# Weight-row requests placed one product later, from the input products to the first projection

## The chip, the cores and the metric

The kernel runs on one core of a Trainium2 chip. The metric is device time of one execution, in microseconds (us), as the median of several runs. A profile is one execution recorded by the hardware's profiler: when every instruction of every engine began, how long it took and which semaphore released it. Engines are named as in the profile: PE is TensorE (matmul), DVE is VectorE, ACT is ScalarE, POOL is GpSimd, SP is SyncE, which here issues nearly all DMAs from one queue.

## The reference

One layer of a hybrid decoder block on x of 1024 tokens by 1024 channels, in float32:

```
xn = rmsnorm(x)
qa, ka, va, qr, kr, vr, gr, gate_a, gate_b = xn @ w_in      (split by columns)
o_a = dilated windowed attention of 12 heads, mixed in 4 slots by their softmax denominators
o_r = groupnorm(retention(qr, kr, vr)) * silu(gr)
y   = sigmoid(gate_a) * (o_a @ w_proj_a) + sigmoid(gate_b) * (o_r @ w_proj_b)
x   = x + y @ w_out
x   = x + square(relu(rmsnorm(x) @ w_up)) @ w_down
```

Everything is to float32 accuracy, so each matmul of two float32 operands is made as three: each operand is split into a high part (a rounded copy) and a low part (the rest), and high x high, high x low and low x high are summed in PSUM.

## The kernel before

The stages follow one another in time: the values (`w_av`), the input products (36 units of `w_in`: 12 of query/key columns, 8 of the retention's gate, 8 of the mixers' gates, 8 of the retention's query/key columns), with the attention of the 12 heads woven into the second half of them; retention, 4 heads of 8 chunks each, with `w_rv`; the first projection (`w_pa`), 16 items, two for each of 8 weight units; the second (`w_pb`), 8 units; `w_out`; the MLP up and down.

**Products.** A unit of the input weight is a matrix of 1024 by 256, multiplied by a form of Strassen's algorithm: seven products N1 to N7, each 12 matmuls of 128x128 by 128x512 (four row blocks times three). They need four pieces of the unit: A (for N1 and N2), B (N6, N3), C (N5, N7) and D (N4). `strassen_order` (L364) lists the products; in the steady part unit j has N6(j), N1(j+2), N5(j), N7(j), N2(j+2), N4(j), N3(j).

**Weights.** Class `Weights` (L68) carries all weights from memory to split pieces. A *row* is one request of 512 KB (256 KB for `w_pa`) into a raw place of SBUF; there are three or four places, taken in turn (`place`). A *step* is one split of a raw row, or a part of it, into high and low part: a copy on ACT (L431) and a subtraction on DVE (L434). A unit has two rows. Its steps are A from the first row, D from the second, four sums of quarters within the raw rows (L159), then B from the first row and C from the second; B and C are the last users of their rows, and mark them in `used`. Over the units the order of steps is A(j+1), D(j), B(j), C(j) (L164 to L174).

**When a step is traced.** `Pipe.step` traces a product's matmuls and then calls `tick` (L304), which counts the clock up and, with `pace` 1, takes one step through `pump` (L270). A step is taken only if the pieces that were in its buffer before are done (`free` marks them after their last product), if its row was requested, and if the clock stands at least `lag` ticks after that row's request (`born`, L278). After each step `pump` calls `load` (L251) until it says no. `load` requests the next row in order if the row that had its place before is in `used`. The product's evacuations from PSUM, and the stores they lead to, are traced after the tick.

In retention, `pace` is None: steps are taken when a weight is freed, in the last chunk of each head, whose product is longer (24 matmuls). From the end of the last chunk on, `lag` is 2 and `pace` 1 again (L1392). In the first projection a tick comes after each of the 16 items: 12 matmuls, then a pinned sigmoid of the next item's gate (L1412), the multiplication of the gate with the sum in PSUM (L1413) and a store (L1414). The item's sum takes one of three banks (`ms`). `split_halves` and `load_half` bring in the operands of the second projection meanwhile.

**What sets the order on the engines.** The PE's order is the program's. For the others a planner of the compiler places the instructions in a simulated time: it takes what it holds to be ready, the earlier traced first. An instruction passed to `keep_in_program_order` is pinned: it is issued behind the instruction that was traced just before it on its engine. Pinned are, among others, the attention's fetches on SP (`late`, L1015: L1023, L1030, L1032, L1046, and L552) and the sigmoids of the gates on ACT (L1215). Requests of rows (L265) are not pinned. A queue is in order: an instruction of SP that waits for a semaphore holds what is behind it.

Of the kernel before, what the change touches and what calls it, by code (L numbers as in the profile page):

```python
# [67 lines left out]
class Weights:  # L68
# [12 lines left out]

    def __init__(self, nc, rawp, wp, split):
        self.nc, self.rawp, self.wp, self.split = nc, rawp, wp, split
        self.raw, self.used, self.next = [], set(), 0
        self.src, self.steps = [], []
        self.place, self.more = [], None
        self.last = {}
        self.units, self.done = {}, set()
        self.plain = self.taken = 0
        self.cycle, self.turn = tuple(range(self.WB)), 0  # L90

        self.places = {}
        self.limit, self.keep, self.first = None, None, {}
        self.clock, self.lag, self.pace, self.every, self.born = 0, 0, None, 1, []

    def claim(self, buf, key):

# [10 lines left out]
    def add(self, src, buf=None, pin=False):  # L108

        n = self.plain  # L110
        if buf is None:
            buf = self.cycle[self.turn % self.WB]
            self.turn += 1
        r = len(self.src)
        self.src.append(src)
        self.place.append(n % 6 if n < 8 else (n - 4) % self.RAW)
        w = src.shape[1]
        cuts = [slice(0, w // 2), slice(w // 2, w)] if n < 3 else [slice(0, w)]

        def step():  # L120
            h, l = self.buffer(buf)
            for c in cuts:
                self.split(h[:, c], l[:, c], self.raw[r][:, c], pin)
            self.units[n] = h, l
            self.used.add(r)

        self.steps.append((self.claim(buf, n), r, step))
        self.plain += 1

    def add_units(self, tag, srcs, flip=0):  # L130

        base = len(self.src)
        self.first[tag] = len(self.steps)
        kept = {}
        for s in srcs:
            self.place += [(len(self.src) + i - base) % (self.RAW + 1) for i in range(2)]
            self.src += [s[1], s[0]]

        def piece(key, buf, r, cols, then=None):
            def step():  # L140
                if isinstance(buf, tuple):
                    if not kept:
                        kept["D"] = self.buffer(buf[0])
                    h, l = (x[:, 512 * buf[1]:512 * buf[1] + 512] for x in kept["D"])
                else:
                    h, l = self.buffer(buf)
                late = key[0] == "pb" and key[1] > 1
                self.split(h, l, self.raw[r][:, cols], late or key[0] == "up" and key[1] < 2 and key[2] != "A")
                self.units[key] = h, l
                if then:  # L150
                    then()

            self.steps.append((self.claim(buf, key), r, step))

        def sums(r, which=(0, 1, 2, 3)):
            (x22, x21), (x11, x12) = ((self.raw[i][:, 0:512], self.raw[i][:, 512:1024]) for i in (r, r - 1))
            for k in which:
                x, y = ((x22, x21), (x21, x11), (x11, x22), (x12, x11))[k]
                ins = self.nc.vector.tensor_tensor(x, x, y, op=OP.add)  # L159
                if tag == "up" and r <= base + 3:  # L160
                    self.keep(ins)

        both = slice(0, 1024)
        for j in range(-1, len(srcs)):  # L164
            if j + 1 < len(srcs):
                piece((tag, j + 1, "A"), self.A[(j + 1) % 2], base + 2 * (j + 1), both)
            if j >= 0:
                r = base + 2 * j + 1
                fine = tag == "pb" and j > 1
                piece((tag, j, "D"), (self.D, j % 2), r, slice(0, 512), None if fine else lambda r=r: sums(r))  # L170
                if fine:
                    self.steps += [(set(), r, lambda r=r, k=k: sums(r, k)) for k in ((0, 1), (2, 3))]
                piece((tag, j, "B"), self.B[(j + flip) % 2], r - 1, both, lambda r=r: self.used.add(r - 1))
                piece((tag, j, "C"), self.C, r, both, lambda r=r: self.used.add(r))  # L174
        m = len(srcs) + flip
        self.cycle = (0, 1, self.B[m % 2], self.C, self.D, self.B[(m - 1) % 2])
        self.turn = 0

    def add_values(self, tag, quarters):

        base = len(self.src)
        w11, w12, w21, w22 = quarters
        self.src += [w[h] for h in range(2) for w in (w22, w21, w11)] + [*w12, *w22]
        self.place += [0, 1, 2, 3, 4, 5, 0, 3, 1, 4]

        def add(x, y):
            self.nc.vector.tensor_tensor(self.raw[x], self.raw[x], self.raw[y], op=OP.add)

        def piece(name, h, buf, r, ends=(), plus=None):
            key = (tag, name, h)  # L190

            def step():
                if plus is not None:
                    add(r, plus)
                hl = self.buffer(buf)
                self.split(*hl, self.raw[r])
                self.units[key] = hl
                self.used.update(ends)

            self.steps.append((self.claim(buf, key), r, step))  # L200

        rows = [range(base + 3 * h, base + 3 * h + 3) for h in range(2)]
        for r22, r21, r11 in rows:
            for x, y in ((r22, r21), (r21, r11), (r11, r22)):
                self.steps.append((set(), r11, lambda x=x, y=y: add(x, y)))
        for h, (r22, r21, r11) in enumerate(rows):
            piece("N6", h, 2 + h, r11)
        for h, (r22, r21, r11) in enumerate(rows):
            piece("N5", h, 4 + h, r22, (r22,))
        for h, (r22, r21, r11) in enumerate(rows):  # L210
            piece("N7", h, h, r21, (r21,))
        for h, (r22, r21, r11) in enumerate(rows):
            piece("N3", h, 2 + h, base + 6 + h, (base + 6 + h, r11), r11)
        for h in range(2):
            piece("N4", h, 4 + h, base + 8 + h, (base + 8 + h,))

    def add_chunks(self, tag, srcs, buffers):


        for c, quarters in enumerate(srcs):  # L220
            base = len(self.src)
            self.place += [(base + i) % (self.RAW + 1) for i in range(4)]
            self.src += quarters
            x00, x10, x11, x01 = range(base, base + 4)
            for name, r, other, op, ends in (
                    ("N1", x00, None, None, ()), ("N2", x10, None, None, ()), ("N3", x11, None, None, ()),
                    ("N5", x00, x01, OP.subtract, ()), ("N7", x01, x11, OP.subtract, (x01,)),
                    ("N6", x11, x00, OP.add, (x00,)), ("N4", x10, x11, OP.subtract, (x10, x11))):
                buf, key = buffers[c % 2][name], (tag, c, name)

                def combine(r=r, other=other, op=op, pin=c > 0):
                    ins = self.nc.vector.tensor_tensor(self.raw[r], self.raw[r], self.raw[other], op=op)
                    if pin:
                        self.keep(ins)

                def step(r=r, ends=ends, buf=buf, key=key, pin=c > 0):
                    h, l = self.buffer(buf)
                    self.split(h, l, self.raw[r], pin)
                    self.units[key] = h, l
                    self.used.update(ends)  # L240

                if other is not None:
                    self.steps.append((set(), x01, combine))
                self.steps.append((self.claim(buf, key), x01, step))
# [6 lines left out]
    def load(self, queues=None):  # L251
# [1 line left out]
        if n >= min(len(self.src), self.hold):  # L253
            return False
        b = self.place[n]
        if any(self.place[m] == b and m not in self.used for m in range(max(0, n - 12), n)):
            return False
        if b >= self.RAW and self.more is None:
            return False
# [30 lines left out]

    def __getitem__(self, i):
        while i not in self.units:
            lag, self.lag, at = self.lag, 0, self.next
            self.pump(1)
            self.lag = lag
            assert self.next > at
        return self.units[i]

# [5 lines left out]
    def tick(self):  # L304
        self.clock += 1
        if self.pace is not None and self.clock % self.every == 0:
            self.pump(self.pace)


class Pipe:  # L310
# [67 lines left out]
def hybrid_block(ctx: ExitStack, tc: tile.TileContext, a: dict, out: bass.AP):  # L378
# [727 lines left out]
    with ExitStack() as ph:  # L1106
# [77 lines left out]

        unit = {}
        NIN = NA + NG + NQ + 8
        W.lag, W.pace = 2, 1
        first = W.take(4)
        for p, (j, name) in enumerate(strassen_order(NIN, True)):
            if p == FIRST - 4:  # L1190
# [204 lines left out]
    with ExitStack() as ph:  # L1395
# [108 lines left out]
        fetched = {order[order.index(at) - 3]: u for at, u in free.items()}  # L1504
        todo, unit, base = [(0, "N3", h) for h in range(2)], {}, len(work)

        W.lag = 3
        fetch(0)
        fetch(1)
        sigmoid(ahead[0][0])  # L1510
# [440 lines left out]
```

## Time and profile before

| | |
|---|---|
| median of 3 runs | 2157.25 us (2156.55 to 2160.52) |
| the profiled execution | 2157.57 us, its span 2155.7 us |
| PE, DVE, ACT, POOL busy | 99%, 64%, 52%, 15% of the span |
| DMA | 366.14 MB, mean 170 GB/s |
| rows requested | 202 (L265) |
| SP's time ahead of row requests, put down to the split on DVE (L434) | 473.0 us, 123 times |

The span runs from the first to the last instruction of the program; the time of the run has some 1.9 us more. A row of a timeline gives the start, the duration, the engine, the line, the operation, what it writes and reads, and in square brackets the idle time before it with what ended it. A row of the waits gives who waited for whom: total, times, longest. A row of the chain of waits gives start, duration and what held the end of the program back at that time. A row of busy time by stage gives the stage, then busy time and number of instructions of PE, PE's weight loads, DVE, ACT, POOL, then the granted clock of PE, the share of the DMA engines and GB/s. All times are in us.

### The profile page before, as it was taken

How to read it: one execution, taken by the hardware profiler on the slowest of the kernel's cores; microseconds unless marked ns; L12 is line 12 of the kernel's file. 1: busy time of each engine (PE TensorE's matmuls, PEld its weight loads, DVE VectorE, ACT ScalarE, POOL GpSimd, SP SyncE). 2: the span in 40 equal slices, each digit the busy share in tenths (PEclk: the TensorE clock that was granted, in tenths of full speed). 3: DMA queues.
4: the chain of work that ended last, by engine and by line, in shares of the span. 5: the costliest groups of instructions: out<-in, count | busy, mean ns of one | idle time of the engine just before them, and what ended most of it. 6: DMA issues, size and time to landing. Idle time of an engine off the chain costs nothing.

```text
span 2155.7 us, 28537 instructions
## 1 busy us (share of the span) xinstructions
PE 2135.5 (99%) x9840; PEld 1751.6 (81%) x9840; DVE 1381.2 (64%) x2352; ACT 1117.2 (52%) x2149; POOL 312.7 (15%) x340
## 2 busy tenths in 40 slices
PE   9999999999999999999999999999999999999999
PEld 7887777888888888888888877778788888788887
DVE  7944434655556565667867777783865556788884
ACT  8534555435555554445555655542655545755552
POOL 1000000000000000003123110000000000777773
PEclk9999999999999999999999999999999999999999
DMA  8433333333667666665354586864254556745443
GB/s 328 152 113 98 109 106 99 106 135 134 197 199 214 196 206 192 209 190 167 110 169 138 156 295 228 277 235 142 84 169 141 155 161 191 238 155 192 159 142 107
DMA packets 296336, 366.14 MB, mean 170 GB/s; under 512 B 35120, under 2 KB 202480, under 8 KB 295936
## 3 DMA queue, kind: packets, MB, share of 16 engines
q1 hardware_dynamic: 295648, 364.06, 53.7%
q8 instruction: 77, 1.26, 0.2%
q14 instruction: 67, 0.55, 0.1%
q10 hardware_dynamic: 544, 0.26, 0.0%
HBM read 247.67 MB, written 116.59 MB: 169 GB/s over the span
## 4 chain that ended last, share of the span: by engine, by line
PE 84%; DVE 5%; DMA 5%; ACT 2%; issue 2%; POOL 1%; SPq 0%; DVEq 0%; POOLq 0%; ACTq 0%
PE mm L327 44%; PE ms L327 32%; PE ms L782 2%; PE tr L997 1%; PE tr L976 1%; PE mm L782 1%; DMA xl<-on_d 1%; DMA s<-sg_d 1%; DVE wl L434 1%; PE tr L987 1%; PE tr L1344 1%; DVE xl L434 1%; PE tr L1129 1%; DVE raw L159 1%; PE ms L1284 1%
## 5 line engine op out<-in xcount | busy, mean ns | idle before, releaser
L434 DVE TENSOR_TENSOR wl<-raw,wh 128x1024 fp32r<-128x1024 f32 (+1 forms) x305 | 338.2, 1110 | 405.2 <-ACT wh L431 404.0
L431 ACT ACTIVATE wh<-raw 128x1024 fp32r<-128x1024 f32 (+1 forms) x305 | 291.6, 959 | 286.0 <-PE ms L327 93.9
L327 PE MATMUL mm<-xh,wh 128*128 128x512 f32 x960 | 388.1, 404 | 3.0 <-ACT ms L504 1.7
L327 PE MATMUL mm<-xh,wl 128*128 128x512 f32 x960 | 375.1, 391 | 0.8 <-DVE wl L434 0.7
L327 PE MATMUL mm<-xl,wh 128*128 128x512 f32 x960 | 374.1, 390 | 0.8 <-DVE xl L434 0.8
L327 PE MATMUL ms<-xh,wh 128*128 128x512 f32 x784 | 318.1, 406 | 4.0 <-ACT u L512 1.6
L327 PE MATMUL ms<-xh,wl 128*128 128x512 f32 x784 | 306.2, 391 | 0.5 <-DVE wl L434 0.5
L327 PE MATMUL ms<-xl,wh 128*128 128x512 f32 x784 | 305.6, 390 | 0.0
L327 PEld LDWEIGHTS mm<-xh,wl 128*128 128x128 f32 x960 | 180.2, 188 | 40.9 <-DVE wl L434 1.9
L327 PEld LDWEIGHTS mm<-xh,wh 128*128 128x128 f32 x960 | 180.5, 188 | 38.8 <-ACT ms L504 2.5
L327 PEld LDWEIGHTS mm<-xl,wh 128*128 128x128 f32 x960 | 180.7, 188 | 35.2 <-DVE xl L434 1.3
L327 PE MATMUL mm<-wh,xh 128*128 128x512 f32 x474 | 192.3, 406 | 0.0
L327 PE MATMUL mm<-wh,xl 128*128 128x512 f32 x474 | 185.6, 392 | 0.0
L327 PE MATMUL mm<-wl,xh 128*128 128x512 f32 x474 | 184.8, 390 | 0.0
L327 PEld LDWEIGHTS ms<-xh,wh 128*128 128x128 f32 x784 | 147.4, 188 | 44.9 <-issue 10.1
L1317 POOL TENSOR_TENSOR st<-st,half 128x1 f32<-128x1 f32 x32 | 25.3, 790 | 1038.6 <-DMA at<-acc_d 882.2
L327 PEld LDWEIGHTS ms<-xh,wl 128*128 128x128 f32 x784 | 147.1, 188 | 32.9 <-DVE wl L434 1.0
L327 PEld LDWEIGHTS ms<-xl,wh 128*128 128x128 f32 x784 | 147.6, 188 | 27.0
L327 PEld LDWEIGHTS mm<-wh,xl 128*128 128x128 f32 x474 | 89.0, 188 | 19.9
L327 PEld LDWEIGHTS mm<-wh,xh 128*128 128x128 f32 x474 | 89.2, 188 | 16.6 <-ACT ms L1761 0.6
L327 PEld LDWEIGHTS mm<-wl,xh 128*128 128x128 f32 x474 | 89.4, 189 | 16.2
L159 DVE TENSOR_TENSOR raw<-raw,raw 128x512 f32<-128x512 f32 x120 | 83.6, 697 | 3.0
(360 smaller groups left out, 3822.0 us busy)
## 6 DMA issues: line engine op xcount, KB each, us to landing
raw<-in_w_up SPq DMA_DIRECT2D x32, 512.0 KB
h_d<-s SPq DMA_DIRECT2D x64, 256.0 KB
raw<-in_w_down SPq DMA_DIRECT2D x32, 512.0 KB
xl<-on_d SPq DMA_DIRECT2D x28, 512.0 KB
raw<-in_w_aqk_q SPq DMA_DIRECT2D x24, 512.0 KB
qk_d<-sg SPq DMA_DIRECT2D x48, 256.0 KB
qk<-qk_d SPq DMA_DIRECT2D x24, 512.0 KB
rb<-rs_d SPq DMA_DIRECT2D x24, 512.0 KB
```

Of the source, the lines that this page charges most:

```text
L159: ins = self.nc.vector.tensor_tensor(x, x, y, op=OP.add)
L327: self.nc.tensor.matmul(ps, x, y, start=start, stop=stop, skip_group_check=not first)
L431: hi = nc.scalar.activation(dst_h, src, AF.Copy)
L434: lo = nc.vector.tensor_tensor(dst_l, src, dst_h.bitcast(F), op=OP.subtract)
L782: nc.tensor.matmul(pm, x, w, start=k == m == 0, stop=k == n - 1 and m == 2)
L976: nc.tensor.matmul(sp[:, to], q, qk[c][:, 1, (n0 - 4 * c) * P:(n1 - 4 * c) * P], start=True, stop=True)
L987: nc.tensor.transpose(tp[:, j], st["p"][:, j * P:(j + 1) * P], ident)
L997: nc.tensor.matmul(po, st["t"][:, j], V[k // 2][:, k % 2], start=(j == 0), stop=(j == nk - 1))
L1129: nc.tensor.matmul(to[m:m + 32], pick[:, 31 - n:63 - n], x, start=n == 0, stop=n == HEADS - 1)
L1284: nc.tensor.matmul(sp[:, :P], kT[:, f], qT[:, f], start=(f == 0), stop=(f == 1))
L1317: nc.gpsimd.tensor_tensor(st[:, 9:10], st[:, 8:9], half[:, 0:1], op=OP.pow)
L1344: nc.tensor.transpose(pt[:, f, :], it["o"][:, f * P:(f + 1) * P], ident)
```

## The change

`Weights` gets a number `rest`. `used`, which was a set of rows whose last split was traced, becomes a table of the clock at which that was (`spent`). `load` asks for the next row only when `rest` ticks have passed since the row ahead of it in its place was used up; a row still in use counts as never. `tick` requests rows after its pump as long as `rest` is not 0 and `load` grants them, since no step need follow to call it. A weight that is needed at once (`__getitem__`) sets `rest` aside, as it does `lag`. `rest` is 1 from the first input product on and 0 again from the second projection on; it is 0 before.

```
     def __init__(self, nc, rawp, wp, split):
-        self.raw, self.used, self.next = [], set(), 0
+        self.raw, self.used, self.next, self.rest = [], {}, 0, 0
...
+    def spent(self, *rs):
+        self.used.update((r, self.clock) for r in rs)
...
-            self.used.add(r)
+            self.spent(r)
...
-        if any(self.place[m] == b and m not in self.used for m in range(max(0, n - 12), n)):
+        if any(self.place[m] == b and self.used.get(m, 1 << 30) + self.rest > self.clock
+               for m in range(max(0, n - 12), n)):
             return False
...
     def __getitem__(self, i):
         while i not in self.units:
-            lag, self.lag, at = self.lag, 0, self.next
+            lag, rest, self.lag, self.rest, at = self.lag, self.rest, 0, 0, self.next
             self.pump(1)
-            self.lag = lag
+            self.lag, self.rest = lag, rest
             assert self.next > at
...
         if self.pace is not None and self.clock % self.every == 0:
             self.pump(self.pace)
+        while self.rest and self.load():
+            pass
...
         NIN = NA + NG + NQ + 8
-        W.lag, W.pace = 2, 1
+        W.lag, W.pace, W.rest = 2, 1, 1
...
-        W.lag = 3
+        W.lag, W.rest = 3, 0
         fetch(0)
```

The other four places that marked a row in `used` call `spent` in the same way.

More of the change, by code (lines that the diff above doesn't have):

```diff
@@ L172, in add_units @@
                     self.steps += [(set(), r, lambda r=r, k=k: sums(r, k)) for k in ((0, 1), (2, 3))]
-                piece((tag, j, "B"), self.B[(j + flip) % 2], r - 1, both, lambda r=r: self.used.add(r - 1))
-                piece((tag, j, "C"), self.C, r, both, lambda r=r: self.used.add(r))
+                piece((tag, j, "B"), self.B[(j + flip) % 2], r - 1, both, lambda r=r: self.spent(r - 1))
+                piece((tag, j, "C"), self.C, r, both, lambda r=r: self.spent(r))
         m = len(srcs) + flip
@@ L197, in step @@
                 self.units[key] = hl
-                self.used.update(ends)
+                self.spent(*ends)
             self.steps.append((self.claim(buf, key), r, step))
@@ L239, in step @@
                     self.units[key] = h, l
-                    self.used.update(ends)
+                    self.spent(*ends)
                 if other is not None:
```

## The prediction

> **What bounds the kernel now.** First the page's totals: TensorE is busy in 99% of the span, so time can only come from the 1% in which it waits.
>
> ```profile
> span 2155.7 us, 28537 instructions
> PE 2135.5 (99%) x9840; PEld 1751.6 (81%) x9840; DVE 1381.2 (64%) x2352; ACT 1117.2 (52%) x2149; POOL 312.7 (15%) x340
> ```
>
> Then the busy time by stage (the first pair after the span is TensorE). The change acts from the input products (about 130 us) to the start of the second projection (about 1286 us).
>
> ```profile
> 130.00:414.00 284.00, 283.95 (x1284) 223.56 (x1283) 124.63 (x157) 146.15 (x207) 0.00 (x0) 1.00 0.35 105
> 414.00:525.00 111.00, 111.00 (x493) 91.94 (x492) 68.77 (x92) 45.50 (x65) 0.00 (x0) 1.00 0.37 125
> 525.00:905.00 380.00, 378.29 (x1925) 318.68 (x1924) 226.52 (x615) 202.51 (x549) 0.00 (x0) 1.00 0.67 204
> 905.00:1225.00 320.00, 318.84 (x1548) 264.07 (x1547) 227.69 (x525) 169.15 (x356) 64.55 (x80) 1.00 0.51 149
> 1225.00:1286.00 61.00, 60.14 (x269) 48.27 (x267) 43.22 (x68) 34.96 (x57) 11.98 (x17) 1.00 0.88 290
> 1286.00:1440.00 154.00, 148.87 (x647) 120.98 (x648) 121.29 (x157) 80.43 (x112) 0.00 (x0) 1.00 0.76 253
> ```
>
> TensorE is idle 0.05 us in the products alone, 1.7 us where attention is woven in, 1.2 us in retention, and at the seam of the two projections. Third, what ended TensorE's waits: the waits of 525 to 905 us (two rows), of retention (one row), and of the seam, 1225 to 1310 us (three rows).
>
> ```profile
> PE tr L976 <- DVE acc L979: 1.4, 1, 1.4
> PE tr L976 <- DVE qk L1040: 0.3, 1, 0.3
> PE tr L1344 <- DVE on L1319: 1.1, 3, 0.6
> PE mm L327 <- ACT wh L431: 1.0, 1, 1.0
> PE mm L327 <- ACT ms L504: 0.8, 1, 0.8
> PE mm L327 <- DVE wl L434: 0.7, 1, 0.7
> ```
>
> So all that could be won in the touched stages is 1.4 + 0.3 + 1.1 + 1.0 + 0.8 + 0.7 = 5.3 us, 0.25% of the span. A loss has no such limit.
>
> **The change, part by part.** No instruction is added or removed: 94 of the 202 requests (`L265`) are traced later: 18 of the query/key rows, 16 each of `w_gr`, `w_gate`, `w_rqk` and `w_rv`, 8 of `w_pa`, 4 of `w_pb`. Each keeps its issue time on SP.
>
> *1. The products.* Counting from the code, unit j has the products N6(j), N1(j+2), N5(j), N7(j), N2(j+2), N4(j), N3(j). At the tick of N6(j) the split B(j+1) is traced and frees a place; the row for A(j+3) is requested there. At the tick of N2(j+2) the same holds for C(j+1) and the second row of unit j+3. The first request moves to the tick of N1(j+2), the second to that of N4(j). The split A(j+3) is traced at N4(j)'s tick, 5 products after its request, now 4; the lag of two ticks does not bind, so no split moves. Here is ACT (two rows), DVE and SP in one such stretch:
>
> ```profile
> 210.88 1.06 ACT L431 ACTIVATE wh<-raw 128x1024 fp32r<-128x1024 f32 x1 [1.62 <-DMA raw<-in_w_aqk_q]
> 216.06 0.58 ACT L512 ACTIVATE u<-ms 128x512 f32<-128x512 f32 x1
> 206.21 1.22 DVE L434 TENSOR_TENSOR wl<-raw,wh 128x1024 fp32r<-128x1024 f32 x1 [1.19 <-ACT wh L431]
> 207.46 10.31 SPq L265 DMA_DIRECT2D raw<-in_w_aqk_q  x2
> ```
>
> SP issues the request 0.03 us after B's split ends (206.21 + 1.22 = 207.43); the row has landed by 210.88, 3.4 us later. And ACT runs the split A, which is traced at N4's tick, before the copy of N7 (216.06), which is traced earlier. So the planner sends an instruction off when it expects it to be ready; its place in the program is only its rank among ready ones, except for those pinned behind the instruction traced before them. With SP idle at 207.43 the request should go out there with the later rank too. If it did wait for its new place, one product costs 2.72 us:
>
> ```profile
> 154.51 2.72 PE mm L327 x12
> ```
>
> A's row would then land 3.4 us after a request 16.3 us (6 products) ahead of N1(j+3), instead of 19.0 us (7 products). That cover hides it. The second row has more: its first use, D(j+3), is traced 8 products on. Taken: 0. If the cover were gone, the same 2.72 us per unit would show, 36 units, 98 us; nothing in these rows comes near that.
>
> *2. The products with attention.* Here the fetches of `V`, `qk`, `rb` and `bias` are pinned, each behind what was traced before it on SP. A request just ahead of one holds it until the split that frees the place. SP, 600 to 612 us:
>
> ```profile
> 601.45 0.55 SPq L1032 DMA_DIRECT2D rb<-rs_d  x1
> 609.06 0.34 SPq L265 DMA_DIRECT2D raw<-in_w_gate_q  x1
> 610.04 0.42 SPq L1046 DMA_DIRECT2D V<-v_d  x1
> ```
>
> SP stands from 602.0 to 609.06 before the request, and `V` goes out behind it at 610.04. The moved request passes the pinned fetches and stores of one product, at most four issues of 0.4 to 0.6 us, some 2 us; they gain up to the 7 us. But TensorE waits only 1.7 us in this stage, and its 1.4 us wait goes back to `rb`, which took 7.56 us to land:
>
> ```profile
> 825.21 7.56 DMA rb<-rs_d
> 824.13 0.37 SPq L1002 DMA_DIRECT2D acc_d<-acc  x1
> ```
>
> What stood ahead of that `rb` on SP was a store of `acc`, with no weight request between. Taken: 0; ends -1.7 (both waits gone) and +2.8 (two more of the 1.4 kind).
>
> *3. Retention.* The requests inside a head's last chunk move to its tick. All splits keep their place, and the 1.1 us of waits are on the group norm's DVE work. Taken: 0, ends -1.1 and +1.1.
>
> *4. The first projection.* Here a tick is one of 16 items, and the lag does bind. The rows of units 3, 4, 5 are requested in the last chunk of retention, now at its tick, one later; so with the lag the split of unit 3 moves from item 0 to item 1, and those up to unit 7 follow (item 4 to item 5). Four `w_pb` rows are requested behind unit 7's split: item 4, now item 6 (one for the split, one for the rest). Their first split, A0, moves from item 6 to item 8, the next from 7 to 9. Each item n also traces, after its tick, the pinned sigmoid of gate n+1. ACT, SP and DVE now:
>
> ```profile
> 1248.02 1.16 ACT L1215 ACTIVATE s<-s 128x512 f32<-128x512 f32 x2
> 1258.58 1.06 ACT L431 ACTIVATE wh<-raw 128x1024 fp32r<-128x1024 f32 x1 [9.40 <-DMA raw<-in_w_pb_q]
> 1259.55 0.61 ACT L1215 ACTIVATE s<-s 128x512 f32<-128x512 f32 x1
> 1253.67 4.83 DMA raw<-in_w_pb_q
> 1254.94 0.69 DVE L1413 TENSOR_TENSOR s<-s,ms 128x512 f32<-128x512 f32 x1 [2.03 <-PE ms L327]
> 1262.29 0.68 DVE L1413 TENSOR_TENSOR s<-s,ms 128x512 f32<-128x512 f32 x1
> 1282.67 0.68 DVE L1413 TENSOR_TENSOR s<-s,ms 128x512 f32<-128x512 f32 x1
> ```
>
> The sigmoids of gates 5 and 6 run, then ACT stands 9.4 us behind A0's row, the sigmoid of gate 7 pinned behind it. So item 6 is multiplied at 1254.94, item 7 at 1262.29 instead of about 1257.7, and item 15 at 1282.67 instead of 1254.94 + 9 x 2.72 = 1279.4. From there the chain of waits runs on:
>
> ```profile
> 1283.38 3.66 DMA pa_d<-s
> 1287.05 5.42 DMA s<-sg_d
> 1292.58 0.64 ACT s L1215
> 1294.39 1.04 ACT L431 ACTIVATE wh<-raw 128x1024 fp32r<-128x1024 f32 x1
> 1295.48 0.50 PE L327 MATMUL mm<-xh,wh 128*128 128x512 f32 x1 [0.99 <-ACT wh L431]
> ```
>
> With A0 ranked after item 8's tick, the sigmoids of 7 and 8 go ahead of it. The items then keep TensorE's pace, item 15 is multiplied up to 3.3 us earlier, the sigmoid at 1292.58 comes near 1289.3, and the weight split at 1294.39 is in time: 1.0 + 0.7 us of waits go. What is late next is the copy `L504` (0.8 us), behind splits on ACT that wait for other loads; I leave it. Taken: -1.7; best -2.5. A0's own cover: TensorE needs it when item 15 ends, 1279.4, and it would run near 1261.
>
> **Sum** against the profiled execution: 2157.57 (span 2155.7 + 1.9 around it) - 1.7 = 2155.9. The median is 0.3 below that execution, so 2155.6 against the median.
>
> **The rivals.**
> *No effect:* the planner sends the requests when it did, and A0 still blocks ACT. For it: 207.46 right behind 207.43. Against: A0's split and the sigmoids change ranks, and these are pinned. 2157.3.
>
> *More comes free:* the held fetches of attention too, the whole seam, and the two waits on ACT in the second projection, 1.6 (`u L512`) and 1.1 (`wh L431`):
>
> ```profile
> PE ms L327 <- ACT u L512: 1.6, 1, 1.6
> PE ms L327 <- ACT wh L431: 1.1, 1, 1.1
> ```
>
> -1.7 - 2.5 - 2.7 = -6.9, 2150.4. Against: TensorE runs unbroken for stretches between the seam and those two.
>
> *Slower, by A0's row coming too late:* the request, two items later, falls behind the `xl<-on_d` loads and gate loads, and A0 blocks ACT again, further on and longer. The projection's pool has three PSUM banks: items 7 to 9 fill them by 1254.94 + 3 x 2.72 = 1263.1, and item 7's is free at 1262.29 + 0.68 = 1262.97. So the 9.4 us are carried with 0.1 to spare, and from there on each microsecond counts. Price at two items: 5.4, 2162.7. Against: two sigmoids more are ahead of it, so ACT reaches it later.
>
> *Slower, by landings in attention:* the window moves 204 GB/s there, and ACT has waited for a row 11 times:
>
> ```profile
> ACT wh L431 <- DMA raw<-in_w_rqk_q: 10.6, 6, 2.9
> ACT wh L431 <- DMA raw<-in_w_gate_q: 6.6, 5, 1.9
> ```
>
> If each of the 11 grew by 2.72 us, and a sixth of that reached TensorE's transposes, 5 us: 2162.2. [...]
>
> **How the numbers follow.** About 0.2%, 4.3 us, is what a measurement of this kernel can tell from no change. Forecast 0.42 (own range 2153 to 2157.5), no effect 0.20, more comes free 0.18, A0 late 0.11, attention late 0.09. Below 2152.9 lie most of the second rival and a tail of the forecast: faster 0.21. Above 2161.6 most of the last two: slower 0.17. Within: 0.62. The range leaves out the far ends of the last three rivals: 2150.5 to 2161.5.
>
> **What would show it.** The same 28537 instructions. Step 1: no idle TensorE from 130 to 525 us, and requests within 3 us of the split before them. Step 2: `V` fetched ahead of the request beside it, 1 to 2 us idle. Step 4: the 9.4 us wait of ACT gone or under 5, item 7 multiplied near 1258, the waits 1.0 and 0.7 gone. Wrong if TensorE waits for `wl` or `wh` before 1225 us, if the seam waits more than 2.5 us, or if a stage behind the change differs by over 2 us.

## The result, and the profile after

The changed kernel takes 2163.38 us (median of 22 runs, 2158.65 to 2168.02) where the kernel before takes 2157.61 (22 runs beside them, 2153.52 to 2163.31): a ratio of 1.0025, 95% interval 1.0019 to 1.0031, so 5.8 us (4.1 to 6.7) slower. The forecast was 2155.6 in a range up to 2161.5. Both the sign and the range were wrong. One execution of run e4 below took 4359.89 us, twice as long as any other, and is in none of the numbers here.

The page of the changed kernel, totals: the execution profiled took 2160.49 us.

```profile
span 2158.6 us, 28540 instructions
PE 2136.5 (99%) x9840; PEld 1752.9 (81%) x9840; DVE 1381.5 (64%) x2352; ACT 1115.3 (52%) x2149; POOL 314.0 (15%) x340
```

The engines have the same counts as before (the three more instructions of the span are none of theirs). This one execution lies at the low end of its kernel's runs, and differs from that of before by 2.9 us only. The busy time by stage, three rows (columns as in the prediction):

```profile
130.00:414.00 284.00, 284.00 (x1285) 223.72 (x1285) 124.79 (x157) 146.10 (x207) 0.00 (x0) 1.00 0.35 105
525.00:905.00 380.00, 376.90 (x1915) 317.20 (x1915) 226.60 (x615) 201.78 (x548) 0.00 (x0) 1.00 0.66 203
1225.00:1286.00 61.00, 59.49 (x266) 47.79 (x265) 41.77 (x65) 32.15 (x53) 15.51 (x19) 1.00 0.84 278
```

TensorE never waits in the products alone; it is idle 3.1 us with attention (1.7 before) and 1.5 us in the seam (0.9 before). What ended TensorE's waits in the changed kernel, 525 to 905 us (the first two rows) and 1225 to 1310 us (four rows); columns: total, times, longest:

```profile
PE tr L982 <- DVE qk L1046: 1.7, 1, 1.7
PE tr L982 <- ACT acc L1006: 1.0, 1, 1.0
PE ms L333 <- DVE s L1419: 1.5, 1, 1.5
PE mm L333 <- ACT wh L437: 1.5, 1, 1.5
PE mm L333 <- ACT ms L510: 1.0, 1, 1.0
PE mm L333 <- DVE wl L440: 0.5, 1, 0.5
```

(The lines of the changed kernel are those of before plus 3 to 6: L265 is now L269, L431 L437, L976 L982, L1040 L1046, L1413 L1419. In runs whose edit adds a line they are one more.) Before, the largest waits of these stages were 1.4 for `acc`, and 1.0, 0.8 and 0.7 at the start of the second projection. New are 1.7 for `qk`, 1.0 for `acc` on ACT, and 1.5 for item 7's multiply.

**Where in the program the time went.** TensorE runs the same 9840 instructions in the same order in all these kernels, so the time between the starts of two given matmuls can be compared from run to run. There are four profiles of the order of before (the one shown, and three repeats told of below) and three of the changed kernel. In us, against the mean of the four:

| stage (times of the first profile of before) | spread of the four | changed, three profiles | mean |
|---|---|---|---|
| start to 524.8 | -1.3 to +1.5 | -1.2, +0.8, -0.8 | -0.4 |
| to 658.9 | -0.2 to +0.3 | +1.7, +2.8, +4.0 | +2.8 |
| to 925.6 | -0.4 to +0.4 | +0.4, +0.6, +1.7 | +0.9 |
| retention, to 1249.2 | -0.1 to +0.3 | -0.2, +0.3, +0.4 | +0.2 |
| seam, to 1281.4 | -0.2 to +0.2 | +1.9, +1.8, +1.7 | +1.8 |
| start of the second projection, to 1307.8 | -1.3 to +1.1 | +1.7, -0.9, -0.6 | +0.1 |
| to the end | -1.0 to +1.3 | -3.2, -2.6, -0.1 | -2.0 |

Two stages stand well clear of the spread: the first stretch of attention (2.8) and the seam (1.8). The second stretch of attention (0.9) does so less surely, since one of its three values is inside the spread and a run told of below, with the order of before in this stretch, has +1.1 there. Two values hold a stretch of half clock, told of at the end and worth some 1.7 us by the estimate there: the +4.0 of the third profile to 658.9 (mean clock 0.57 from 541 to 545 us), and the +1.7 of the first at the start of the second projection (0.58 from 1300 to 1304 us). Attention, seam and retention make 5.7 us. Over the whole span the three profiles stand 3.4 us above the four. The -2.0 of the last stage falls at a few places (near 1386, 1420, 1836 and 1960 us) where the waits of the four differ by 1 to 2.4 us as well; it is left unexplained. The first and the last two stages differ by several us between executions of one and the same kernel, which is why a single pair of profiles shows 2.9 us where the medians differ by 5.8.

**Attention, 525 to 540 us.** What stands in another order from here on: on SP seven row requests of attention and retention go out two to nine places later, behind pinned fetches and loads; with them four splits of rows on ACT and three on DVE, and little else; up to 525 us no engine's order differs. Here is the first of the seven. The kernel before, timeline (SP three rows, ACT one):

```profile
525.58 0.33 SPq L265 DMA_DIRECT2D raw<-in_w_gate_q  x1
525.96 0.56 SPq L1030 DMA_DIRECT2D qk<-qk_d  x1
526.57 0.59 SPq L1032 DMA_DIRECT2D rb<-rs_d  x1
529.29 1.04 ACT L431 ACTIVATE wh<-raw 128x1024 fp32r<-128x1024 f32 x1
```

The row is asked for just ahead of 1 MB of `qk` and `rb`, which wait behind it; its split on ACT runs 3.7 us later and waits for nothing. The changed kernel, timeline of SP (three rows), ACT (two), DVE and PE:

```profile
524.06 0.56 SPq L1036 DMA_DIRECT2D qk<-qk_d  x1
524.73 0.55 SPq L1038 DMA_DIRECT2D rb<-rs_d  x1
525.88 0.41 SPq L269 DMA_DIRECT2D raw<-in_w_gate_q  x1
532.35 1.06 ACT L437 ACTIVATE wh<-raw 128x1024 fp32r<-128x1024 f32 x1 [2.84 <-DMA raw<-in_w_gate_q]
536.70 0.63 ACT L1181 ACTIVATE sg<-u 128x512 f32<-128x512 f32 x1
537.98 1.41 DVE L1046 SCALAR_TENSOR_TENSOR qk<-qk,gqk,rb 128x512 f32<-128x512 f32 x2
539.44 0.49 PE L982 MATMUL tr<-qk 128*128 128x128 f32 x2 [1.74 <-DVE qk L1046]
```

The row is asked for only 0.3 us later on the clock, but the 1 MB and one 128 KB fetch of `V` are in front of it now, and it has landed 6.45 us after its request (532.33). ACT is in order and stands 2.84 us for it; behind it are the sigmoid of the gate product, on DVE the product with it, and pinned behind that the scaling of `qk`. TensorE comes to the scores at 537.7 and waits 1.74 us.

**The seam.** The changed kernel, timeline of ACT (three rows), DVE (four), GpSimd (two), SP (three), PE:

```profile
1249.68 1.15 ACT L1221 ACTIVATE s<-s 128x512 f32<-128x512 f32 x2
1251.67 0.63 ACT L1221 ACTIVATE s<-s 128x512 f32<-128x512 f32 x1
1263.15 1.06 ACT L437 ACTIVATE wh<-raw 128x1024 fp32r<-128x1024 f32 x1 [9.90 <-DMA raw<-in_w_pb_q]
1251.81 3.24 DVE L440 TENSOR_TENSOR xl<-xl,xh 128x1024 fp32r<-128x1024 f32 x2
1256.53 0.69 DVE L1419 TENSOR_TENSOR s<-s,ms 128x512 f32<-128x512 f32 x1 [0.88 <-PE ms L333]
1264.24 1.23 DVE L440 TENSOR_TENSOR wl<-raw,wh 128x1024 fp32r<-128x1024 f32 x1 [7.03 <-ACT wh L437]
1265.39 0.68 DVE L1419 TENSOR_TENSOR s<-s,ms 128x512 f32<-128x512 f32 x1
1252.25 1.72 POOL L1367 TENSOR_TENSOR onT<-onT 128x256 f32<-128x256 f32 x1
1253.93 1.71 POOL L1366 TENSOR_TENSOR onE<-onE,n 128x256 f32<-128x256 f32 x1
1255.67 0.37 SPq L1345 DMA_DIRECT2D on_d<-onE  x1
1257.29 0.62 SPq L1420 DMA_DIRECT2D pa_d<-s  x1
1258.01 0.40 SPq L269 DMA_DIRECT2D raw<-in_w_pb_q  x1
1266.12 0.50 PE L333 MATMUL ms<-xh,wh 128*128 128x512 f32 x1 [1.47 <-DVE s L1419]
```

Nine sigmoids now run ahead of A0 where seven did: those of gates 7 and 8 came forward, as predicted. But ACT still stands 9.9 us for A0's row, and so does DVE: there the subtraction that makes A0's low part (1264.24) stands ahead of item 7's multiply (1265.39). And the row is asked for later. Against item 6's multiply, which follows TensorE, the request went out 1.27 us ahead before (1253.67 against 1254.94, in the prediction) and 1.48 us behind now (1258.01 against 1256.53): 2.75 us. A store of `pa_d` stands in front of it (0.7 us), and the store of retention's last sums waits for GpSimd, whose last two sums take 1.7 us each. Before:

```profile
1250.59 0.74 POOL L1361 TENSOR_TENSOR onT<-onT 128x256 f32<-128x256 f32 x1
1251.29 0.74 POOL L1360 TENSOR_TENSOR onE<-onE,n 128x256 f32<-128x256 f32 x1
```

They are 1.95 us longer together, beside the two subtractions of the second projection's operands on DVE (1251.81), which the planner put into the room it saw ahead of A0.

### The profile page after: what moved, and what is told of

Same layout as the page of the kernel before. It is cut to its first block, busy times and chain, and to the rows that moved or that the text cites. A ratio compares the mean times of both kernels' runs of the same rounds, so it can differ in the third digit from the quotient of the medians.

```text
span 2158.6 us, 28540 instructions
## 1 busy us (share of the span) xinstructions
PE 2136.5 (99%) x9840; PEld 1752.9 (81%) x9840; DVE 1381.5 (64%) x2352; ACT 1115.3 (52%) x2149; POOL 314.0 (15%) x340
## 4 chain that ended last, share of the span: by engine, by line
PE 81%; DVE 6%; DMA 5%; issue 3%; ACT 2%; POOL 1%; SPq 0%; POOLq 0%; DVEq 0%; ACTq 0%
PE mm L333 43%; PE ms L333 30%; PE ms L788 2%; PE tr L1003 1%; PE tr L982 1%; DVE wl L440 1%; PE mm L788 1%; DMA s<-sg_d 1%; DVE xl L440 1%; ACT wh L437 1%; PE tr L993 1%; DMA raw<-in_w_gate_q 1%; DVE raw L162 1%; PE tr L1350 1%; PE tr L1135 1%
## 5 line engine op out<-in xcount | busy, mean ns | idle before, releaser
L437 ACT ACTIVATE wh<-raw 128x1024 fp32r<-128x1024 f32 (+1 forms) x305 | 291.6, 959 | 292.0 <-PE ms L333 92.2
```

The source lines that it names most:

```text
L437: hi = nc.scalar.activation(dst_h, src, AF.Copy)
```

## The experiments

The theory: the loss comes from these two places, by order alone. The rivals: from one of the two; or from something that the order doesn't hold, spread over the program.

**Each part alone (e1, e2).** The place of before from retention on, set where the input products end; and the reverse, `rest` 0 up to that line and 1 from it:

```
-        W.lag, W.pace = 1, None
+        W.lag, W.pace, W.rest = 1, None, 0
```

> The later place holds in the input products only (rest is 0 again from retention on). My theory: the loss has two sources that the orders on SP, ACT and DVE show, seven requests in attention that go out behind the fetches of qk and rb, and the seam of the two projections; this run has the first alone. In attention TensorE waits some 2.9 us instead of 1.7, by the change's one profile, and the seam stands as before (longest wait there 1.0 us): 1.5 to 3 us over the kernel before. Rival, the loss is in the seam alone: within 1 us of the kernel before. Rival, the loss is not in these orders but spread over the program: about half or more of 5.8 us, with waits of TensorE that neither stage holds.

> The later place holds from the end of the input products on only: retention and first projection. Nothing moves on any engine before the seam. My theory: A0's row is requested about 2.7 us later against TensorE's own progress, because the subtractions of two operands of the second projection run beside GpSimd's last sums of retention; TensorE waits about 1.5 us near 1264 for the multiply of item 7, and the waits at the start of the second projection grow by some 1 us: 2 to 4 us over the kernel before, of which up to 2 are given back later. Rival, the loss is in attention alone: within 1 us. The two parts alone should add up to the whole, 5.8 us; if they add up to under 4, something is in their sum.

Products only: 2161.19 us (12 runs), 1.0016 of before (1.0006 to 1.0027), 3.5 us. Seam only: 2159.49 (12 runs), 1.0013 (1.0004 to 1.0022), 2.8 us. Both rivals of a single place fall, the one against the seam narrowly (its interval begins at 0.9 us). The parts add up to the whole within their intervals, 6.3 against 5.4 by the ratios. Not all came as expected: products only lies above its 1.5 to 3 us, and with the seam only the waits at the start of the second projection did not grow by 1 us, they are 1.6 us where before has 2.5. By the matmuls, products only has +2.3 us in 525 to 659, +1.4 to 926 and -0.3 in the seam; seam only has -0.2 in 525 to 659 and +1.7 in the seam. (It has +1.1 in 659 to 926 as well, where its order is that of before: so large can chance be there.)

**The seam (e3, e4): who holds item 7, and why the request is late.** First, one instruction of the changed kernel moved: A0's low part on DVE behind item 7's multiply.

```
+                with self.behind() if key == ("pb", 0, "A") else ExitStack():
                     self.split(h, l, self.raw[r][:, cols], ...)
...
+            ins = nc.vector.tensor_tensor(gates[n], gates[n], pp, op=OP.mult)
+            if n == 7:
+                W.behind = lambda: tc.issue_after(ins7)
+                ins7 = ins.ins
```

> The changed kernel with one instruction moved: on DVE the subtraction that makes A0's low part stands behind the multiply of item 7 instead of ahead of it. My theory: with the sigmoids of gates 7 and 8 now ahead of A0 on ACT, it is DVE's queue that holds item 7 (its multiply ran at 1265.39, behind that subtraction that waited 7.03 us for A0's high part). Item 7 is then multiplied near 1259.3, the 1.47 us wait at 1266.12 is gone, item 8 is the one that waits, without TensorE: 1.5 us less than the changed kernel, about 2161.9. Rival, the banks fill one item later all the same: no difference to 2163.4, with the wait some 2.7 us later.

Its timeline, DVE:

```profile
1260.27 0.69 DVE L1420 TENSOR_TENSOR s<-s,ms 128x512 f32<-128x512 f32 x1 [2.04 <-PE ms L334]
1265.16 1.22 DVE L441 TENSOR_TENSOR wl<-raw,wh 128x1024 fp32r<-128x1024 f32 x1 [4.20 <-ACT wh L438]
```

Item 7 is multiplied when TensorE has it, at 1260.27, 4.9 us ahead of A0's low part, and the wait of 1.47 us is 0.1. The seam is 0.3 us from before, no longer 1.8. So it was DVE's queue that held item 7. The time does not settle it: 2161.93 (12 runs) is the expected median, but against the runs of before beside it the ratio is 1.0027 (1.0018 to 1.0037), where some 1.0018 was expected. The interval just allows that; the profile has a wait of 1.3 us at the start of the second projection again.

Second, the splits of the second projection's operands two items later, so that none stands ahead of A0:

```
-            split_halves(n - 4)
+            split_halves(n - 4 if n > 9 else n - 6)
```

> The changed kernel, with the splits of the second projection's operands two items later up to item 9, so that none stands ahead of A0's split. My theory: the two subtractions on DVE at 1251.81 are what makes GpSimd's last two sums take 1.7 us instead of 0.74; without them the sums take 0.74, their store goes out 2 us earlier, and A0's row is requested near 1256 and lands near 1261: the wait of 1.47 us goes to about 0, 1 to 2 us less than the changed kernel (2161.4 to 2162.4). Rival, the store of item 4 ahead of the request is what makes it late: the sums shorten or not, the request comes within 0.7 us of where it is, and the wait stays over 0.8 us. Rival, GpSimd's longer sums come from something else: they stay at 1.7 us.

Its timeline, GpSimd, SP, DVE (item 6):

```profile
1254.34 0.73 POOL L1367 TENSOR_TENSOR onT<-onT 128x256 f32<-128x256 f32 x1
1255.02 0.74 POOL L1366 TENSOR_TENSOR onE<-onE,n 128x256 f32<-128x256 f32 x1
1258.12 0.40 SPq L269 DMA_DIRECT2D raw<-in_w_pb_q  x1
1258.69 0.69 DVE L1419 TENSOR_TENSOR s<-s,ms 128x512 f32<-128x512 f32 x1 [2.10 <-PE ms L333]
```

Without the subtractions beside them the sums take 0.74 us again. The request is 0.57 us ahead of item 6, 2.05 earlier than in the changed kernel; the 0.7 us that it is behind before is the store in front. TensorE does not wait between 1240 and 1285 us, though A0's low part stands ahead of item 7 as before: with the row in time the three banks carry it. Time: 2161.74 (11 runs), 1.0020 (1.0011 to 1.0030). That is 1.6 us under the changed kernel by the medians and 1.1 by the ratios, as expected, but the two intervals overlap, so it is the trace that shows the gain and not the time. Of the rivals, the store alone falls, and so does another cause of GpSimd's longer sums.

**Attention (e5, e6): one row, and the queue.** The later place for the one gate row of 525 us:

```
+        rest = self.rest if n == 62 else 0
-        ... self.used.get(m, 1 << 30) + self.rest > self.clock
+        ... self.used.get(m, 1 << 30) + rest > self.clock
```

> The later place for one row alone, the gate row that before was requested at 525.58, just ahead of the fetches of qk and rb; all other rows keep the place of before. One instruction moves on SP (three places back), one on ACT and one on DVE. My theory: this one row makes the 1.7 to 2.5 us wait of TensorE near 539, since it lands some 6 us after its request behind 1 MB of qk and rb, ACT's queue stands for it, and the silu and the scaling of qk come 1.5 us late; so the stretch from 525 to 659 us is 2 us longer and nothing else: 1.5 to 2.5 us over the kernel before. Rival, the wait near 539 has several causes (other rows of attention, later): under 1 us, the wait under 1 us.

Its timeline, SP, ACT, PE:

```profile
528.19 0.41 SPq L270 DMA_DIRECT2D raw<-in_w_gate_q  x1
534.87 1.06 ACT L438 ACTIVATE wh<-raw 128x1024 fp32r<-128x1024 f32 x1 [2.98 <-DMA raw<-in_w_gate_q]
541.96 0.49 PE L983 MATMUL tr<-qk 128*128 128x128 f32 x2 [1.88 <-DVE qk L1047]
```

One instruction moved on SP, one on ACT, one on DVE, and the wait is there (1.88 us), the row 6.7 us after its request. The time: 2160.88 (12 runs), 1.0014 (1.0005 to 1.0023), 3 us, above the 1.5 to 2.5 expected; by the matmuls the stretch of 525 to 659 is 1.3 us longer, about what the wait adds, and the other 1.7 us of the time have no place in the trace that the order explains.

Then the same row at the same place, issued from ACT's own queue, so that `qk` and `rb` are not ahead of it in its queue:

```
+        queues = queues or [self.nc.scalar if n == 62 else self.nc.sync]
```

> The same one row, asked for at the later place, but issued from ACT's own queue, so that the fetches of qk and rb are not ahead of it in its queue, while they still move at the same time. Everything else stands in the order of before. My theory in its first form (a row behind 1 MB in the same queue waits for that MB): it lands 3.5 to 4.5 us after its issue, and the wait near 539 is at most 0.4 us: the same time as before. Rival, the bytes of qk, rb and the row share the same DMA engines whatever the queue: it lands 5.5 us or more after its issue, and 1 to 2 us of the wait stay.

Its timeline, SP, ACT's queue, ACT:

```profile
525.21 0.56 SPq L1037 DMA_DIRECT2D qk<-qk_d  x1
525.87 0.55 SPq L1039 DMA_DIRECT2D rb<-rs_d  x1
526.83 0.47 ACTq L270 DMA_DIRECT2D raw<-in_w_gate_q  x1
534.57 2.00 ACT L438 ACTIVATE wh<-raw 128x1024 fp32r<-128x1024 f32 x2 [3.90 <-DMA raw<-in_w_gate_q]
```

The row lands 7.7 us after its issue, later than from SP, and TensorE waits 3.2 us (1.7 and 1.5). My first form of the theory, that the queue's order holds the row, falls: with 1 MB under way from SP the row is late from another queue too. The rival's landing came (7.7 us, where it said 5.5 or more). That the row and the 1 MB share the DMA engines fits: from 526.5 to 532.5 us the 16 engines are busy for 80% of the time or more; but no view shows which engine moved which bytes, so the sharing is inferred. What the order on SP did before was to send the row out 0.38 us ahead of `qk` and 0.99 us ahead of `rb`. The landing is what this run shows; the length of the wait is not as clean, since the issue took a place on ACT, and a copy of `ms` there (L511), which stood ahead of a step of the softmax before, came behind it. Time: 2160.02 (11 runs), 1.0009 (0.9999 to 1.0019), which does not tell it from the kernel before.

**The seam mended alone, and both places undone (e7 to e10).** First the seam of e4 with the attention of before:

> The later place from retention on only, and the operands' splits of the second projection two items later up to item 9: the seam of e4 with the attention of before. My theory: no wait near 1265, the sigmoids of gates 7 and 8 ahead of A0, the waits at 1286 to 1297 1 us instead of 2.5: 1 to 2 us under the kernel before, about 2156, which is what step 4 of the prediction took. Rival, the seam's gain is given back by the second projection's waits at 1386 and 1420, or is lost in their spread: within 0.5 us of the kernel before.

2157.13 us (12 runs), 0.9996 (0.9987 to 1.0006): the loss of the seam is gone, but there is no gain. TensorE's waits, 1225 to 1310 us:

```profile
PE mm L333 <- ACT wh L437: 1.4, 1, 1.4
PE mm L333 <- ACT ms L510: 1.2, 1, 1.2
PE mm L333 <- DVE wl L440: 0.5, 1, 0.5
```

The wait on item 7 is gone; those at the start of the second projection were expected to fall to 1 us and are 3.1, not less than before (2.5). So the rival has the time right but not the road: nothing was given back at 1386 or 1420, since the gain never came. This kernel is the best of the new ones, and the same as before.

Then the changed kernel with both places undone (the gate row of 525 at its place of before, the operands later):

> The changed kernel with its two places of loss undone and all else kept: the one gate row of 525 us keeps its place of before, and the operands' splits come two items later up to item 9. Six rows of attention still go out behind their fetches, and A0 is still ranked two items later. My theory: these two places are the whole loss; the waits near 539 and 1265 are at most 0.4 us, and the time is within 0.1% of the kernel before (ratio 0.999 to 1.001). Rival, the other six rows cost as well: the wait near 778 stays at 0.4 to 1 us, attention is 1 us or more longer, ratio 1.001 or above.

The two waits are gone, and the one near 778 stays at 0.8 us; by the matmuls 525 to 926 us is 0.9 us longer and the seam 0.3 shorter. The time says more: 2159.83 (11 runs), 1.0014 (1.0003 to 1.0025). So the two places are not the whole. Two runs to settle that, the six other moved rows alone and the same kernel again:

> The later place in the input products only, for all rows but the gate row of 525 us; the seam as before. If the six other moved rows of attention cost what the trace of the run with both places undone shows (a wait of 0.4 to 0.8 us near 778, half a microsecond between 659 and 774 us): ratio 1.0000 to 1.0007. Rival, they cost what the time of that run shows: 1.0010 to 1.0018, with waits of over 1 us in attention in its profile.

> The changed kernel with both places undone, once more: same program as before, a second time and a second profile. By the trace some 0.5 to 1 us over the kernel before, ratio 1.0002 to 1.0005; by its first time 1.0014. The wait near 778 comes again, at 0.4 to 1 us; those near 539 and 1265 stay at most 0.4 us.

Six rows: 2160.27 (12 runs), 1.0013 (1.0004 to 1.0021). Again: 2160.78 (11 runs), 1.0013 (1.0004 to 1.0021). By the time the rival holds: the six rows cost some 3 us (0.9 to 4.5). TensorE's waits with the six rows, 525 to 905 us:

```profile
PE tr L983 <- DVE acc L986: 1.7, 3, 1.0
PE tr L1004 <- ACT acc L1007: 0.8, 1, 0.8
```

TensorE waits at changing places, 778, 837, 855, 889 us here, 660 and 837 us in the other, where the wait near 778 did not come again; 525 to 926 us is 3.3 and 2.3 us longer. Each is under 1.2 us, and which of them come differs from execution to execution, unlike the wait at 539.

Not all of these are the work of the six rows. The matmul near 837 waits in all four profiles of the order of before as well (0.2 to 1.4 us), and 1.2 us in the run with the seam only. Only the wait near 778 goes with the moved rows: eight of the nine profiles that move the six have it (0.4 to 1.0 us), and with the six in their old place the longest is 0.15. In the changed kernel's first profile ACT stands 4.12 us there for a row of `w_rqk` (2.14 before), ahead of a copy that TensorE needs. So the cost of the six rows is shown by three times, and by the traces in part only.

**Repeats (n1 to n5).** The changed kernel with `rest` at 0 throughout is the program of before; it was run three times, twice with times:

> The changed kernel with rest at 0 from the first product on, so that no request moves: every engine has the order of the kernel before. A null run, for the question why medians differ by 5.8 us where one profile of each differs by 2.9. If the loss is in the orders: same as before within the interval, ratio 1.000 (0.999 to 1.001). If a part of it comes from how a changed kernel is built or timed: 1 to 3 us slower. Its profile is a second one of the program of before: the 1.64 us wait on ACT at 1386 and the 1.4 us wait at 834 either come again or were of that one execution.

> The program of before a third time, for its profile: by the theory no wait over 0.5 us near 539, 778 or 1266 again.

> The null run once more, orders of before: 0.999 to 1.001. With the first (1.0004) it says how far a ratio of this size is from no change.

2158.53 (11 runs), 1.0004 (0.9995 to 1.0014), and 2157.06 (12 runs), 1.0002 (0.9993 to 1.0010). No change, so the loss is in the orders. A single ratio of 1.0013 is only just told from that: the first null's interval reaches 1.0014. In the three profiles TensorE waits 0.3 us near 539 and never near 778 or 1266; the waits of 1.4 (834) and 1.6 us (1386) of the first profile of before are 0.2 to 0.4 and 0 to 1.7 in these. The changed kernel, two profiles more:

> The changed kernel once more, for a second profile. My theory (orders in attention and in the seam): TensorE waits some 1.7 us near 539, 0.5 to 1 us near 778, about 1.4 us near 1266 and near 1299 again, since these follow from order; what lies behind 1400 us differs from execution to execution by up to 1 us a wait. Rival, the waits of attention are chance landings: one of them is gone, or another as long stands elsewhere.

> The changed kernel a third time, for its profile: as the second.

2.5 and 2.1 us near 539, 0.4 and 0.4 near 778, 1.4 and 1.3 near 1266: these three follow from the order. The 1.5 us near 1299 does not: 0.2 and 0.4.

What stays open is the exact split. One row 1.0014, six rows 1.0013, seam 1.0013: the sum is more than the whole, 1.0025, and each is known to within some 0.0009.

## Why the prediction was wrong, point by point

*Step 1, the products: right.* No order changes and TensorE does not wait. The planner sent the requests when it had, and the later rank was absorbed.

*Step 2, attention: the term that failed.* "The moved request passes the pinned fetches and stores of one product, at most four issues of 0.4 to 0.6 us, some 2 us". I priced a place in SP's queue by the time that SP needs to issue. On the clock the request was only 0.3 us later. What it passed were 1 MB of transfers, and passing them cost the row its landing: 6.45 us where 3.7 was enough. The gain that I set against it, fetches that come up to 7 us earlier, was worth nothing, since only one wait of before hung on them. Taken 0, ends -1.7 and +2.8; measured 3.7 us (2.8 and 0.9), some 0.6 of it from the half clock in one of the three profiles. The rival of landings in attention had the side and nearly the size (5 us, chance 0.09), with a wrong road there: it let all rows grow alike and a sixth reach TensorE. ACT's waits for these rows grew from 17.2 us (15.3 to 16.5 in the three repeats) to 23.2 (23.5 and 23.3), as two rows of ACT's waits in the changed kernel, 525 to 905 us, show:

```profile
ACT wh L437 <- DMA raw<-in_w_rqk_q: 13.2, 6, 4.1
ACT wh L437 <- DMA raw<-in_w_gate_q: 10.0, 6, 3.0
```

Of these 6.0 us one row brought TensorE a wait of 1.7 to 2.5 us, and another the wait near 778 (0.4 to 1.0). Through which waits the six other rows cost the 3 us of their times is open. I held that rival for unlikely because 17.2 us of such waits had not reached TensorE. The row of 525 us shows why they had not: the order of before kept it ahead of the fetches.

*Step 3, retention: right.* +0.2 us, waits 1.1 us as before.

*Step 4, the first projection: wrong in sign.* That A0 is ranked two items later and the sigmoids of 7 and 8 go ahead held. "The items then keep TensorE's pace" did not, since I followed ACT alone. A split has two halves; the low part on DVE was still ahead of item 7's multiply, and the run with that one instruction moved showed it. Second, the room ahead of A0 did not stay empty: two operand splits moved in, slowed GpSimd's sums by 1.95 us, and with the store in front the request came 2.75 us later. I had worked out that the banks carried the stall "with 0.1 to spare", and from there on each microsecond counted: 1.47. That is the rival of A0's row coming too late (chance 0.11, 5.4 us); measured 1.8. Its road was another: the request fell behind stores, one of them waiting for GpSimd, and not behind the loads of `xl` and the gates. Two signs that the prediction named failed with it: ACT's 9.4 us wait, forecast gone or under 5, is 9.9, and the seam waits 4.5 us in all, over the 2.5 named. The expected -1.7 was not there either. From item 6 to item 15 is 27.7 us before (1254.94 to 1282.67) and 27.0 to 27.1 in the three repeats of it, 29.2 in the changed kernel, 27.1 with item 7 first (1257.55 to 1284.67) and 26.8 with the operands later. So taking item 7 out of A0's way gives nothing that the repeats of before do not give, where 3.3 us was forecast; the sigmoids of three later gates wait 1.1 to 1.2 us each for their loads in that run.

*The sum.* -1.7 + 0 + 0 + 0 was taken; +1.8 + 3.7 + 0.2 + 0 came, 5.7 us, against a difference of medians of 5.8. That the two agree so closely is partly luck: over their whole spans the same profiles differ by 3.4. Two rivals that I held for unlikely came true together; I had them exclude each other and gave each its chance alone.

## What to carry to other kernels

A request moved past another is to be priced by the bytes that it lets go ahead, and not by the issue slots alone (here a request 0.3 us later, behind 1 MB, landed 6.45 us after its issue, where 3.7 us was enough before): look which engine in order waits for its landing (here ACT, 2.84 us), and what stands behind that. When work is moved out of a queue's way, follow each of its instructions on each engine, and ask what the planner puts into the room (here two subtractions, with GpSimd's sums 1.95 us longer). Before a change of a few us is read from traces, take several profiles of each kernel, and compare the time between the same two instructions.

## What the runs showed that I had not expected

**A wait of TensorE can cost more than its length.** Busy time by stage of the changed kernel, the third-last column the granted clock:

```profile
1300.00:1304.00 4.00, 3.47 (x9) 2.57 (x9) 3.64 (x5) 0.00 (x0) 0.00 (x0) 0.58 0.82 214
```

After the waits of 1.5 and 0.5 us that end at 1300.8 the mean clock of these 4 us is 0.58, and nine matmuls run in 3.47 busy us where the product of the prediction's row (12 in 2.72 us) would have 15. The second profile of the changed kernel (n2), behind its wait of 2.5 us that ends at 542.8:

```profile
543.00:547.00 4.00, 4.00 (x21) 3.39 (x21) 2.45 (x6) 3.61 (x9) 0.00 (x0) 1.00 0.49 158
```

There it is not. Over the 17 profiles of this case, from 60 us on and taking waits within 3 us of each other together: of 33 with 1.5 us or more of idle time, 11 were followed by such a stretch (the shortest had 1.6 us), of some 200 with 0.3 to 1.5 us, none. A stretch costs some 1.7 us, an estimate: the clock records of the traces give each 3.41 us at 0.5. The clock's changes stand on a grid: the records of the kernel before and of the changed one have 2150.40, 1293.65 and 853.33 us from one change to the next, 630, 379 and 250 times 3.4133 us. Cut into pieces of that length on the grid, the first profile of the changed kernel has 1.95 us of idle TensorE in the piece from 1297.26 to 1300.68, and half clock follows; 1.74 us from 536.09 to 539.50 is not followed by it, nor is 1.48 us in the profile of before (1419.33 to 1422.74). How much idle time it takes is not settled by that: the 1.6 us above was enough in another profile.

**Two subtractions on DVE beside two sums on GpSimd.** The two subtractions at 1251.81 took 3.24 us, GpSimd's sums beside them 1.72 and 1.71 instead of 0.74. In e4, with no such subtraction beside them, the sums take 0.73 and 0.74 us. The subtractions were slowed as well, from 2.35 us. From the start of the first subtraction to the end of the last sum is 3.83 us (1251.81 to 1255.64), as much as two subtractions (2.35) and two sums (0.74 each) take one after the other; why, no view shows. Two subtractions without GpSimd, in the same profile:

```profile
1268.85 2.35 DVE L440 TENSOR_TENSOR xl<-xl,xh 128x1024 fp32r<-128x1024 f32 x2
```
